# Sums of squares on TensorE and lo parts on VectorE in the opening of a hybrid RWKV-7/FoX trunk kernel

## The chip, the core and the metric

The kernel runs on one core of one Trainium2 chip. A core has a matrix engine (TensorE, "PE"; its weight loads are listed apart as "PEld"), a vector engine (VectorE, "DVE"), an engine for activation functions (ScalarE, "ACT"), a general engine (GpSimd, "POOL") and an engine that mostly issues DMAs (SyncE, "SP"). Each engine works through its own list of instructions in order, and they wait for each other through semaphores. The metric is the time of one execution on the device, in microseconds.

All matrix products with weights are made to nearly fp32 accuracy out of three products of a faster format, fp32r. An operand is split into a high part, `hi` (the value rounded to fp32r, a copy on ScalarE), and a low part, `lo` (the value less `hi`, a subtraction on VectorE or GpSimd); then `hi*hi + hi*lo + lo*hi` is summed up in PSUM. Operands that are plain fp32 go through TensorE in another way, in which each product is recorded as two.

## The reference, cut to what matters

One layer: 16 meta tokens are put ahead of 512 tokens of width 1024; the combined input projection feeds an RWKV-7 group, a forgetting-attention group (FoX) and the gates.

```python
h = jnp.concatenate([meta_b, x], axis=1)              # 528 x 1024
u = rmsnorm(h, norm_mix[l])                           # h * rsqrt(mean(h*h) + 1e-6) * g
proj = u @ w_in[l]
feat_rw, feat_fx = proj[..., :C_RW], proj[..., C_RW:C_RW + C_FX]
...
# RWKV-7, after the token shift: r, k, v, wd, ad (64 + 64 columns), gd (128 columns)
w_log = -jax.nn.softplus(-(w0 + jnp.tanh(wd) @ w_lora_up)) - DECAY_OFFSET
a = jax.nn.sigmoid(a0 + ad @ a_lora_up)
g = jax.nn.sigmoid(gd) @ g_lora_up
...
# FoX: fl are 8 columns, one for each head
F = jnp.cumsum(jax.nn.log_sigmoid(fl + b_f))
```

The opening computes the sums of squares for `rmsnorm`, the feature blocks wd/ad ("LoRA block") and gd ("gate LoRA block"), the eight forget columns and their cumulative sum F, and the normalised `u` as hi and lo part for all projections that follow. Behind it come the recurrence, the attention, the output projections and an MLP.

## The kernel before

The activations stand transposed: 1024 channels as 8 blocks of 128 partitions (`k`), and the 528 tokens as two halves of 264 (`t`). The input arrives as `xt[t]`, four pieces of two channel blocks each (`c`), by SP's DMA queue, with the weights of the two LoRA blocks (`wraw`) queued between them.

For each half t the opening does the following.

- For each piece c: ScalarE squares it into `sq` (L340; three buffers). For its two channel blocks ScalarE makes `uhi`, the gained but not yet normalised value (L343), and VectorE makes `ulo` (L344). VectorE adds the two squares up into `acc` (L347 for the first piece, L350 twice for each other one).
- TensorE forms `pf`, the eight forget columns, from `uhi`, `ulo` and the split weights `wf` (L355, 24 products). Then it multiplies `acc` with a matrix of ones, so that every partition gets the sum over all channels (`pss`, L358, one plain fp32 product).
- ScalarE makes the reciprocal root `rs` out of it, by Ln and Exp (L360, L361). VectorE scales `pf` by it into `f0` (L363).
- `proj(B_LORA, ...)` multiplies the half with the LoRA weights (L293, 24 products into a `pj` buffer; there are two). The evacuation scales by `rs` (L369), makes a scaled copy `tm` on ScalarE (L306) and combines them in the token shift into `lf` (L307).

Then `proj(B_GD, ...)` does the same for the gate LoRA block, both halves. After that the normalised values replace the others: VectorE scales `xt` (L379), ScalarE casts it into `uhi` (L381), VectorE subtracts (`ulo`, L382).

The forget columns go through bias, log-sigmoid and a cumulative scan (L395 to L401) into `fF`, which is stored to `fF_d` (L402) and later read by the attention (`nF`). `fF` shares its buffer with `lc`, the scan of the first decay (L693); `f0` shares that of `tha`. Then the LoRA features get tanh (L407) and the gate features a sigmoid by tanh (L408, L409), and both are split into `lhi` and `llo` (L261, called from the lines behind). The first decay uses `lhi` and `llo` of the LoRA block in TensorE's products L688.

ScalarE's functions come in tables: Ln and Exp lie in one, tanh in another, and each change is an instruction ACT_TABLE_LOAD.

After the opening a planner written in Python (`Clock`, `Turns`) interleaves the streams: recurrence, attention, FoX features, and, as filler, the projections of 40 blocks. It estimates when operands are ready and sets TensorE's order by that; the other engines' order is set by a scheduler with priorities. `projections` fetches a block's weights (L440), splits them in `convert` (hi on ScalarE, L449; lo on GpSimd, L450), and multiplies (L478, 24 products for each half into a `pj` buffer, of which there are two). The first blocks are those of the first pair's keys (`okk`) and receptances (`orr`); the sums for the keys' norm are L710. A `pj` buffer is free again when `tm` (L306) and the token shift (L307) have read it.

`load_w(src, low)` fetches two halves of a block and splits them through `load_h`; `low` says which engine makes the two lo parts, and without it that is VectorE. For the two LoRA blocks `(G, G)` is given: GpSimd, L237.

Of the kernel before, what the change touches and what calls it, by code (L numbers as in the profile page):

```python
# [9 lines left out]
F32 = mybir.dt.float32  # L10
# [3 lines left out]
AF = mybir.ActivationFunctionType  # L14
ALU = mybir.AluOpType
# [4 lines left out]
T = 528  # L20
# [5 lines left out]
HT = T // 2  # L26
# [22 lines left out]
B_LORA = 0  # L49
B_GD = 1  # L50
# [138 lines left out]
def kernel(ctx, tc, ht, x, win, par, cst, gain, lora, wout, wo, wup, wdn, out, dbg=None):  # L189
    nc = tc.nc  # L190
    dbg = dbg or {}
    mm = nc.tensor.matmul
    act = nc.scalar.activation
    V, G, A = nc.vector, nc.gpsimd, nc.scalar
# [35 lines left out]
    def load_h(src, low, tag, bufs):  # L230

        raw = wp.tile([128, 512], F32, name=tag + "raw", bufs=bufs[0])
        nc.sync.dma_start(raw, src)
        hi = wp.tile([128, 512], F32R, name=tag + "hi", bufs=bufs[1])
        lo = wp.tile([128, 512], F32R, name=tag + "lo", bufs=bufs[2])
        A.copy(hi, raw)  # L236
        low.tensor_tensor(lo, raw, hi.bitcast(F32), ALU.subtract)  # L237
        return hi, lo

    def load_w(src, low=(V, V)):  # L240

        return [load_h(src[:, 512 * j:512 * j + 512], low[j], "w", (4, 4, 4)) for j in range(2)]

    def wk(w, k):

        return [x[:, 128 * (k % 4):128 * (k % 4) + 128] for x in w[k // 4]]
# [12 lines left out]
    def split(hi, lo, x):  # L259
        A.copy(hi, x)  # L260
        V.tensor_tensor(lo, x, hi.bitcast(F32), ALU.subtract)  # L261

    def passes(w, x):
        return ((w[0], x[0]), (w[0], x[1]), (w[1], x[0]))
# [6 lines left out]
    with ExitStack() as st:  # L271
# [3 lines left out]
        def ppj(name="ppj"):  # L275
            return ps.tile([128, 512], F32, name=name, tag="pj", bufs=2)

        def psm(name="psm"):
            return ps.tile([128, 512], F32, name=name, tag="sm", bufs=4)
# [5 lines left out]
        def proj(blk, evac, parts=((0, HT), (HT, T)), w=None):  # L285

            w = w or load_w(win[blk], (G, V))
            for a0, a1 in parts:
                po = ppj("pj")[:, :a1 - a0]
                n = 0  # L290
                for k in range(KB):
                    for a, b in passes(wk(w, k), U):
                        mm(po, a, b[:, k, a0:a1], start=n == 0, stop=n == 23)  # L293
                        n += 1
                evac(po, slice(a0, a1))
# [4 lines left out]
        def tshift(blk, dst):  # L300

            tm = rp.tile([128, 1 + T], F32, name="tm")
            V.memset(tm[:, 0:1], 0.0)

            def evac(po, sl):
                act(tm[:, sl.start + 1:sl.stop + 1], po, AF.Copy, scale=pr[:, C_MU + blk:C_MU + blk + 1])  # L306
                V.scalar_tensor_tensor(dst[:, sl], po, pr1[:, blk:blk + 1], tm[:, sl], ALU.mult, ALU.add)  # L307
            return evac
# [5 lines left out]
        lhi = cp.tile([128, 2, T], F32R, name="lhi")  # L314
        llo = cp.tile([128, 2, T], F32R, name="llo")
# [2 lines left out]
        f0 = rp.tile([8, T], F32, name="f0", tag="tha")  # L318
        f1 = rp.tile([8, T], F32, name="f1", tag="sq")
        lfs = [rp.tile([128, TP], F32, name=f"lf{i}", tag=("okk", "orr")[i]) for i in range(2)]  # L320
        with tc.tile_pool(name="xp", bufs=2) as xp:
            ones = xp.tile([128, 128], F32, name="ones", bufs=1)
            V.memset(ones, 1.0)
            xt = [yp.tile([128, KB, HT], F32, name=f"xt{t}", tag=("y_rw", "y_fx")[t]) for t in range(2)]
            nc.sync.dma_start(pr, par)
            for c in range(4):
                nc.sync.dma_start(xt[0][:, 2 * c:2 * c + 2, :].rearrange("p a b -> p (a b)"), ht[0, c])
            w_lora = load_w(win[B_LORA], (G, G))
            for c in range(4):
                nc.sync.dma_start(xt[1][:, 2 * c:2 * c + 2, :].rearrange("p a b -> p (a b)"), ht[1, c])  # L330
            w_gd = load_w(win[B_GD], (G, G))
            nc.sync.dma_start(cs, cst)
            wf = [xp.tile([128, 64], F32R, name=f"wf{i}", bufs=1) for i in range(2)]
            split(wf[0], wf[1], pr[:, C_FL:])
            rss = []
            for t in range(2):
                tk = slice(HT * t, HT * t + HT)
                for c in range(4):
                    sq = xp.tile([128, 2, HT], F32, name="sq", bufs=3)
                    act(sq, xt[t][:, 2 * c:2 * c + 2, :], AF.Square)  # L340
                    for k in range(2 * c, 2 * c + 2):
                        gn = pr[:, C_GN + k:C_GN + k + 1]
                        act(uhi[:, k, tk], xt[t][:, k, :], AF.Copy, scale=gn)  # L343
                        V.scalar_tensor_tensor(ulo[:, k, tk], xt[t][:, k, :], gn, uhi[:, k, tk].bitcast(F32), ALU.mult, ALU.subtract)  # L344
                    if c == 0:
                        acc = xp.tile([128, HT], F32, name="acc")
                        V.tensor_tensor(acc, sq[:, 0, :], sq[:, 1, :], ALU.add)  # L347
                    else:
                        for k in range(2):
                            V.tensor_tensor(acc, acc, sq[:, k, :], ALU.add)  # L350
                pf = psm("pf")[:8, :HT]
                n = 0
                for k in range(KB):
                    for a, b in passes([x[:, 8 * k:8 * k + 8] for x in wf], U):
                        mm(pf, a, b[:, k, tk], start=n == 0, stop=n == 23)  # L355
                        n += 1
                pq = psm("pss")[:, :HT]
                mm(pq, ones, acc, start=True, stop=True)  # L358
                rs = xp.tile([128, HT], F32, name="rs")
                act(rs, pq, AF.Ln, bias=eps, scale=1.0 / 1024)  # L360
                act(rs, rs, AF.Exp, scale=-0.5)  # L361
                rss.append(rs)
                V.tensor_tensor(f0[:, tk], pf, rs[:8], ALU.mult)  # L363
                if t == 0:
                    V.tensor_scalar(pr1, pr[:, C_MU:C_MU + 14], -1.0, 1.0, ALU.mult, ALU.add)
                    shift = tshift(12 + B_LORA, lfs[0])

                def normed_shift(po, sl):
                    V.tensor_tensor(po, po, rss[sl.start // HT], ALU.mult)  # L369
                    shift(po, sl)  # L370

                proj(B_LORA, normed_shift, ((tk.start, tk.stop),), w_lora)
            shift = tshift(12 + B_GD, lfs[1])
            proj(B_GD, normed_shift, w=w_gd)
            for t in range(2):
                tk = slice(HT * t, HT * t + HT)
                for c in range(4):
                    for k in range(2 * c, 2 * c + 2):
                        V.scalar_tensor_tensor(xt[t][:, k, :], xt[t][:, k, :], pr[:, C_GN + k:C_GN + k + 1], rss[t], ALU.mult, ALU.mult)  # L379
                    kk = slice(2 * c, 2 * c + 2)  # L380
                    A.copy(uhi[:, kk, tk], xt[t][:, kk, :])  # L381
                    V.tensor_tensor(ulo[:, kk, tk], xt[t][:, kk, :], uhi[:, kk, tk].bitcast(F32), ALU.subtract)  # L382
# [20 lines left out]
        dump("F", fF)  # L403


        lf, gf = (x[:, :T] for x in lfs)
        act(lf[:64], lf[:64], AF.Tanh)  # L407
        act(gf, gf, AF.Tanh, scale=0.5)  # L408
        V.tensor_scalar(gf, gf, 0.5, 0.5, ALU.mult, ALU.add)  # L409
        split(lhi[:, B_LORA, :], llo[:, B_LORA, :], lf)  # L410
        split(lhi[:, B_GD, :], llo[:, B_GD, :], gf)

        fp = st.enter_context(tc.tile_pool(name="fp", bufs=1))
# [22 lines left out]
        def fetch(job):  # L436
# [4 lines left out]
                raws.append(raw)  # L441
            return job, raws

        def convert(job, raws):
            w = []
            for raw in raws:
                hi = wp.tile([128, 512], F32R, name="whi", bufs=4)
                lo = wp.tile([128, 512], F32R, name="wlo", bufs=4)
                A.copy(hi, raw)  # L449
                G.tensor_tensor(lo, raw, hi.bitcast(F32), ALU.subtract)  # L450
                w.append((hi, lo))
            return job, w

# [594 lines left out]
    with ExitStack() as st:  # L1048
# [35 lines left out]
        for j in range(2):  # L1084
            we = yp.tile([128, 2, 2, 512], F32R, name=f"we{j}", tag=("y_rw", "y_fx")[j])
            for x in range(2):
                raw = wp.tile([128, 512], F32, name="wraw", bufs=4)
# [5 lines left out]
        for b2 in range(4):  # L1093
            w = load_w(wo[0, b2])
            for i, b1 in [(i, b1) for b1 in range(2) for i in range(4)] if b2 < 3 else [(i, b1) for i in range(4) for b1 in range(2)]:
                k = 2 * b2 + b1
                for n, (a, b) in enumerate(passes(M, w[b1])):
                    mm(pd[i], a[:, k, 128 * i:128 * i + 128], b, start=k == 0 and n == 0, stop=k == 7 and n == 2)
        for k in range(KB):
            raw = wp.tile([128, 512], F32, name="wraw", bufs=4)  # L1100
# [265 lines left out]
```

## Time and profile before

| | us |
|---|---|
| three runs | 919.47, 911.35, 915.79 |
| their median | 915.79 |
| the profiled execution | 918.31 |
| its span | 916.5 |

Busy over the span: TensorE 860.8 us (94%), VectorE 601.1 (66%), ScalarE 464.6 (51%), GpSimd 187.7 (20%). The granted clock of TensorE has a mean of 0.969 of full speed.

How to read the lines that follow. A line of the timeline gives the start, the time taken, engine, source line, operation, the tile written and those read, shape and count, and in brackets how long the engine had been idle and what ended that. Where a count is over 1, the time is that from the first start to the last end. An instruction may start before the one ahead of it ends, so the step from start to start is the price of one in a dense stretch. A line of the windows gives a stretch and its length, then busy time and number of instructions of PE, PEld, DVE, ACT and POOL, the granted clock of TensorE, the busy share of the DMA engines and GB/s. A line of the groups gives the count, then busy time and mean nanoseconds of one, then the idle time before. The chain of waits gives start, length, and what the time went to.

### The profile page before, as it was taken

Reading aid. Unit: us, or ns where it says so; the run is one execution under the profiler, and the core shown is the slowest. Engines: PE = TensorE matmul, PEld = TensorE weight load, DVE = VectorE, ACT = ScalarE, POOL = GpSimd, SP = SyncE. Lnnn points to the kernel's source line nnn. Section 1 sums busy time; section 2 is a strip of 40 time slices with the busy share of each in tenths; the row PEclk is TensorE's granted clock in tenths of the full one; section 3 lists DMA queues with packets and bytes.
Section 4 is the critical chain, followed back from the end, with each engine's and each line's share of the span. In section 5 each row is a group of like instructions: output and inputs, shape, how many; then the busy total and the mean of one; then the engine's idle time right before and its main releaser. Section 6 shows DMA issues by size and latency. Waiting matters only on the chain.

```text
span 916.5 us, 15714 instructions
## 1 busy us (share of the span) xinstructions
PE 860.8 (94%) x5868; PEld 699.9 (76%) x5868; DVE 601.1 (66%) x1174; ACT 464.6 (51%) x939; POOL 187.7 (20%) x177
## 2 busy tenths in 40 slices
PE   6589897999989899999999999999999999999998
PEld 4587785867887777767867877888888888888886
DVE  7966875555877697465366756467556675566776
ACT  7756342585545443467364645245544454344542
POOL 4253533314533345222401210000000000000000
PEclk9889988999989899999997999999999999999999
DMA  6122634748464546665686644024632356422465
GB/s 209 46 71 70 161 94 136 185 105 209 105 140 117 138 133 188 174 161 138 152 218 218 213 164 128 1 79 131 193 126 93 104 178 194 156 96 101 137 222 170
DMA packets 69772, 129.46 MB, mean 141 GB/s; under 512 B 6840, under 2 KB 7992, under 8 KB 69696
## 3 DMA queue, kind: packets, MB, share of 16 engines
q1 hardware_dynamic: 52288, 94.91, 32.0%
q0 software_dynamic: 8704, 16.78, 11.4%
q10 hardware_dynamic: 8704, 16.78, 5.5%
q8 instruction: 46, 0.75, 0.3%
q14 instruction: 30, 0.25, 0.1%
HBM read 122.13 MB, written 39.86 MB: 177 GB/s over the span
## 4 chain that ended last, share of the span: by engine, by line
PE 72%; DVE 16%; DMA 4%; ACT 4%; issue 3%; POOL 0%; POOLq 0%; SPq 0%; ACTq 0%; DVEq 0%
PE po L1145 19%; PE pj L478 17%; PE po L1235 12%; PE pd L1235 5%; PE po L1066 2%; PE po L1115 2%; DMA wraw<-in_win 2%; PE pw L830 2%; PE py L627 1%; PE psc L582 1%; DVE tmp L812 1%; DVE AX L824 1%; PE pbt L778 1%; DVE xt L379 1%; PE psr L763 1%
## 5 line engine op out<-in xcount | busy, mean ns | idle before, releaser
L237 DVE TENSOR_TENSOR wlo<-wraw,whi 128x512 fp32r<-128x512 f32 x196 | 138.3, 713 | 95.4 <-ACT whi L236 95.3
L236 ACT CAST whi<-wraw 128x512 fp32r<-128x512 f32 x200 | 123.7, 621 | 134.8 <-PE po L1145 43.9
L478 PE MATMUL pj<-uhi,whi 128*128 128x264 f32 (+1 forms) x480 | 170.9, 356 | 10.4 <-ACT gt L489 4.7
L478 PE MATMUL pj<-uhi,wlo 128*128 128x264 f32 (+1 forms) x480 | 158.5, 330 | 0.0
L478 PE MATMUL pj<-ulo,whi 128*128 128x264 f32 (+1 forms) x480 | 158.4, 330 | 0.0
L450 POOL TENSOR_TENSOR wlo<-wraw,whi 128x512 fp32r<-128x512 f32 x80 | 110.3, 1389 | 173.9 <-ACT whi L449 155.4
L478 PEld LDWEIGHTS pj<-uhi,whi 128*128 128x128 f32 x480 | 94.3, 197 | 31.9 <-issue 11.6
L478 PEld LDWEIGHTS pj<-uhi,wlo 128*128 128x128 f32 x480 | 94.7, 197 | 7.2
L478 PEld LDWEIGHTS pj<-ulo,whi 128*128 128x128 f32 x480 | 95.0, 198 | 4.2
L1145 PE MATMUL po<-zhi,whi 128*128 128x512 f32 (+1 forms) x248 | 94.8, 382 | 0.0
L1145 PE MATMUL po<-zlo,whi 128*128 128x512 f32 (+1 forms) x248 | 94.8, 382 | 0.0
L1145 PE MATMUL po<-zhi,wlo 128*128 128x512 f32 (+1 forms) x248 | 94.8, 382 | 0.0
L449 ACT CAST whi<-wraw 128x512 fp32r<-128x512 f32 x80 | 49.4, 618 | 52.4 <-PE pj L478 29.8
L1235 PE MATMUL po<-wlo,fhi 128*128 128x512 f32 x160 | 62.3, 390 | 0.0
L1235 PE MATMUL po<-whi,flo 128*128 128x512 f32 x160 | 62.3, 390 | 0.0
L1235 PE MATMUL po<-whi,fhi 128*128 128x512 f32 x160 | 62.2, 389 | 0.0
L1145 PEld LDWEIGHTS po<-zlo,whi 128*128 128x128 f32 x248 | 46.6, 188 | 9.1
L1145 PEld LDWEIGHTS po<-zhi,wlo 128*128 128x128 f32 x248 | 46.6, 188 | 9.0
L1145 PEld LDWEIGHTS po<-zhi,whi 128*128 128x128 f32 x248 | 46.6, 188 | 9.0
L1157 ACT CAST fhi<-R 128x768 fp32r<-128x768 f32 (+1 forms) x32 | 30.2, 944 | 24.2 <-DVE R L1164 13.6
L1158 DVE TENSOR_TENSOR flo<-R,fhi 128x768 fp32r<-128x768 f32 (+1 forms) x32 | 34.8, 1088 | 7.8 <-ACT fhi L1157 7.8
L1235 PEld LDWEIGHTS po<-wlo,fhi 128*128 128x128 f32 x160 | 30.0, 188 | 6.5 <-DVE wlo L237 0.2
(295 smaller groups left out, 1667.9 us busy)
## 6 DMA issues: line engine op xcount, KB each, us to landing
wraw<-in_win SPq DMA_DIRECT2D x84, 256.0 KB, 3.2
tsum<-in_wdn ACTq DMA_DIRECT2D x32, 512.0 KB, 4.4
wraw<-in_wup SPq DMA_DIRECT2D x64, 256.0 KB, 2.6
wraw<-tsum SPq DMA_DIRECT2D x64, 256.0 KB, 2.8
wraw<-in_wdn SPq DMA_DIRECT2D x48, 256.0 KB, 2.6
tsum<-in_wdn POOLq DMA_DIRECT2D x16, 512.0 KB, 7.4
tsum<-tsum POOLq DMA_DIRECT2D x16, 512.0 KB, 6.7
gd<-gt SPq DMA_DIRECT2D x16, 256.0 KB, 2.4
```

Of the source, the lines that this page charges most:

```text
L236: A.copy(hi, raw)
L237: low.tensor_tensor(lo, raw, hi.bitcast(F32), ALU.subtract)
L449: A.copy(hi, raw)
L450: G.tensor_tensor(lo, raw, hi.bitcast(F32), ALU.subtract)
L478: mm(po, a, b[:, k, a0:a1], start=n == 0, stop=n == 23)
L830: mm(ps_[hs, n - b0, :], lhs(n)[hs], rhs(n)[hs], start=True, stop=True)
L1066: mm(po, a, b[:, k, :], start=n == 0, stop=n == 11)
L1115: mm(po, a[:, k, 128 * i:128 * i + 128], b[:, k, :], start=n == 0, stop=n == 23)
L1145: mm(po[:, t0:t1], a, b[:, k, t0:t1], start=n == 0, stop=n == 23)
L1157: A.copy(fhi[:, j, a:b], R[:, a:b])
L1158: V.tensor_tensor(flo[:, j, a:b], R[:, a:b], fhi[:, j, a:b].bitcast(F32), ALU.subtract)
L1235: mm(x[i], a[:, k, left, 128 * i:128 * i + 128], c, start=start and k == 0 and n == 0, stop=stop and k == n_pairs - 1 and n == 2)
```

## The change

It has three parts.

1. `acc` and its additions are gone. Each square is multiplied with the ones directly and summed up in PSUM: 8 plain fp32 products for each half instead of one, issued behind each piece.
2. The lo parts of the two LoRA blocks' weights and of the first two projection jobs (four tiles each) are made by VectorE instead of GpSimd.
3. Tanh and split of the LoRA features stand ahead of the gate LoRA block instead of behind the cumulative scan.

```diff
@@ opening
+        lf, gf = (x[:, :T] for x in lfs)
...
-            w_lora = load_w(win[B_LORA], (G, G))
+            w_lora = load_w(win[B_LORA])
...
-            w_gd = load_w(win[B_GD], (G, G))
+            w_gd = load_w(win[B_GD])
...
                     if c == 0:
-                        acc = xp.tile([128, HT], F32, name="acc")
-                        V.tensor_tensor(acc, sq[:, 0, :], sq[:, 1, :], ALU.add)
-                    else:
-                        for k in range(2):
-                            V.tensor_tensor(acc, acc, sq[:, k, :], ALU.add)
+                        pq = psm("pss")[:, :HT]
+                    for k in range(2):
+                        mm(pq, ones, sq[:, k, :], start=c + k == 0, stop=c + k == 4)
...
-                pq = psm("pss")[:, :HT]
-                mm(pq, ones, acc, start=True, stop=True)
...
                 proj(B_LORA, normed_shift, ((tk.start, tk.stop),), w_lora)
+            act(lf[:64], lf[:64], AF.Tanh)
+            split(lhi[:, B_LORA, :], llo[:, B_LORA, :], lf)
             shift = tshift(12 + B_GD, lfs[1])
             proj(B_GD, normed_shift, w=w_gd)
@@ behind the cumulative scan
-        lf, gf = (x[:, :T] for x in lfs)
-        act(lf[:64], lf[:64], AF.Tanh)
         act(gf, gf, AF.Tanh, scale=0.5)
         V.tensor_scalar(gf, gf, 0.5, 0.5, ALU.mult, ALU.add)
-        split(lhi[:, B_LORA, :], llo[:, B_LORA, :], lf)
         split(lhi[:, B_GD, :], llo[:, B_GD, :], gf)
@@ projections
+        converted = []
+
         def convert(job, raws):
+            low = V if len(converted) < 2 else G
+            converted.append(job)
...
-                G.tensor_tensor(lo, raw, hi.bitcast(F32), ALU.subtract)
+                low.tensor_tensor(lo, raw, hi.bitcast(F32), ALU.subtract)
```

In the order in which the changed kernel issues, TensorE begins with the six sums of the first three pieces of the first half; then come six pf products, the two sums of the last piece, the other 18 pf products and the LoRA block of that half; then the eight sums, 24 pf products and the LoRA block of the second half; then the gate LoRA block with the L688 products in its last quarter, and L478. On SP the store of `fF` now leaves after six of L440's weight tiles, where it left after eight. ScalarE loads a table three times between the opening's Ln/Exp and the first decay, as before. Past the first decay and the first keys, the lists of all engines are the same in both kernels but for a few neighbours that change places.

## The prediction

> **What bounds the kernel now.** I read the windows of the opening first, then the chain of waits, then each engine's timeline up to 60 us. Times are microseconds from the start of the span. The windows give, for each stretch, the busy time of TensorE (PE), its weight loads (PEld), VectorE (DVE), ScalarE (ACT) and GpSimd (POOL), with counts, and the clock granted to TensorE:
>
> ```profile
> 15.00:20.00 5.00, 3.97 (x34) 3.16 (x33) 4.96 (x10) 5.00 (x12) 2.93 (x2) 1.00 0.27 85
> ...
> 25.00:30.00 5.00, 3.42 (x28) 3.20 (x27) 5.00 (x11) 4.28 (x8) 1.26 (x1) 1.00 0.17 52
> 30.00:35.00 5.00, 2.89 (x23) 2.48 (x21) 5.00 (x12) 4.99 (x10) 1.19 (x1) 1.00 0.01 2
> 35.00:40.00 5.00, 0.00 (x0) 0.00 (x0) 5.00 (x8) 2.11 (x5) 1.79 (x2) 0.75 0.30 105
> 40.00:45.00 5.00, 3.62 (x20) 3.39 (x21) 3.82 (x8) 4.94 (x8) 0.28 (x2) 0.50 0.00 0
> ```
>
> VectorE is full from 15 to 40 us, and TensorE has nothing at all to do in the last five of them; then its clock stands at 0.50. The chain of waits says the same: work of VectorE, one piece after the other, until the split of the LoRA features (L261) lets the first L688 product go:
>
> ```profile
> 10.12 0.52 ACT sq L340
> ...
> 40.09 0.62 DVE ulo L382
> 40.71 0.63 DVE llo L261
> 41.34 0.04 issue
> 41.38 1.47 PE pup L688 x10
> 42.85 11.16 PE pj L478 x72
> ```
>
> So a gain in the opening is worth what it brings forward the stream of L478. Behind the opening all engines of the changed kernel issue in the old order but for a few neighbours, so what is gained there moves the rest as a block.
>
> **What VectorE loses and takes on.** Groups in the first 30 us (count, busy us, mean ns), and from the whole page the subtraction at L237 on VectorE:
>
> ```profile
> L237 POOL TENSOR_TENSOR wlo<-wraw,whi 128x512 fp32r<-128x512 f32 x4 | 5.9, 1506 | 9.4 <-ACT whi L236 9.4
> L350 DVE TENSOR_TENSOR acc<-acc,sq 128x264 f32<-128x264 f32 x12 | 5.1, 428 | 1.3 <-ACT sq L340 1.3
> ...
> L237 DVE TENSOR_TENSOR wlo<-wraw,whi 128x512 fp32r<-128x512 f32 x196 | 138.3, 713 | 95.4 <-ACT whi L236 95.3
> ```
>
> The 14 additions (these twelve and the two of L347, at 0.43: 6.0 us) go. Eight lo parts come: four of L237 and the four of the first two projection jobs, 8 x 0.71 = 5.7 us. On busy time that is nothing. But VectorE is also held up under GpSimd's subtractions:
>
> ```profile
> 17.16 1.91 DVE L344 SCALAR_TENSOR_TENSOR ulo<-xt,pr,uhi 128x264 fp32r<-128x264 f32 x2
> 34.57 2.51 DVE L379 SCALAR_TENSOR_TENSOR xt<-xt,pr,rs 128x264 f32<-128x264 f32 x2
> 37.63 0.48 DVE L379 SCALAR_TENSOR_TENSOR xt<-xt,pr,rs 128x264 f32<-128x264 f32 x1
> ...
> 33.81 2.98 POOL L450 TENSOR_TENSOR wlo<-wraw,whi 128x512 fp32r<-128x512 f32 x2 [7.55 <-ACT whi L449]
> ```
>
> Undisturbed, an instruction takes 0.48; these pairs take 1.91 and 2.51 instead of about 0.9, so 1.0 to 1.6 us are lost each time. With eight subtractions off GpSimd some 5 us of stalls should go too. The Trainium skill, page "SBUF — State Buffer", section "SBUF: two separate sides", has a GpSimd operation and a VectorE one with two SBUF inputs exclude each other for a whole instruction; by that the loss is up to one subtraction each, and these rows agree. VectorE is then no longer the bound, and the question is what is late next.
>
> **What comes next: TensorE.** The sums of squares become 16 plain fp32 products against two before, each recorded as two:
>
> ```profile
> 24.22 0.28 PE L293 MATMUL pj<-ulo,whi 128*128 128x264 f32 x1
> 24.35 0.71 PE L358 MATMUL pss<-acc,ones 128*128 128x264 f32 x2
> 24.71 0.48 PE L293 MATMUL pj<-uhi,wlo 128*128 128x264 f32 x1
> 25.03 0.28 PE L293 MATMUL pj<-uhi,whi 128*128 128x264 f32 x1
> ...
> 47.76 0.28 PE L478 MATMUL pj<-ulo,whi 128*128 128x264 f32 x1
> ...
> 53.72 0.28 PE L478 MATMUL pj<-uhi,wlo 128*128 128x264 f32 x1
> 53.93 1.11 PE L710 MATMUL pkk<-sq,cs 64*64 64x264 f32 x8
> ```
>
> Between 47.76 and 53.72 lie 49 steps of 0.122, the price of one fp32r product. From 24.35 to 25.03 go one sum and one such product, so a sum holds TensorE for 0.68 - 0.12 = 0.56. Bounds: 0.24 (both records at the fp32r pace) and 0.86 (two records of 0.43 one after the other). I take 0.56, the row itself. The Trainium skill, page "FP8 and Floating Point Precision", section "TensorE Precision Notes", counts four passes for true fp32; four times 0.122 is 0.49 as an estimate, and the sum below would be 0.7 us shorter by it.
>
> TensorE's new order is strict: the sums of the first half stand ahead of most of its pf products, those of the second half behind the whole LoRA block of the first half. The last squares of the first half are ready at 10.64, as now (10.12 + 0.52; their input lands no earlier). From there, two sums 1.1; 18 pf products left 2.2; LoRA block 24 x 0.122 = 2.9; eight sums 4.5; pf of the second half 2.9; its LoRA block 2.9; drain 0.3: 27.5. The squares that wait for a free sq buffer (three, now freed by TensorE and not VectorE) are made in time, since the eight sums begin at 16.9.
>
> **Then ScalarE.** From 27.5 its queue is full. These rows price it by start-to-start steps:
>
> ```profile
> 27.67 0.48 ACT L306 ACTIVATE tm<-pj,pr 128x264 f32<-128x264 f32 x1 [0.57 <-DVE pj L369]
> 28.05 0.62 ACT L381 CAST uhi<-xt 128x528 fp32r<-128x528 f32 x1
> 28.57 0.73 ACT L395 ACTIVATE f<-f,pr 8x528 f32<-8x528 f32 x1
> 29.32 1.28 ACT L407 ACT_TABLE_LOAD   x1
> 30.61 0.65 ACT L407 ACTIVATE lf<-lf 64x528 f32<-64x528 f32 x1
> 31.16 0.46 ACT L306 ACTIVATE tm<-pj,pr 128x264 f32<-128x264 f32 x1
> ...
> 40.96 1.28 ACT L398 ACT_TABLE_LOAD   x1
> 42.25 0.64 ACT L398 ACTIVATE f<-f 8x528 f32<-8x528 f32 x1
> ```
>
> VectorE's scaling of the block (0.4) puts the first tm at 27.9. Then, in the changed order: three tm at 0.38, eight uhi casts and the lhi cast at 0.52, one table load 1.29, tanh 0.55, and the first decay's two sg and one small cast, about 1.1 by the tm and cast rows: 8.8. So the load ahead of L398 starts at 36.7 instead of 40.96, 4.3 earlier. The tanh and split moved ahead cost nothing of their own: three table loads before, three after. Its cover is that TensorE meanwhile does the second LoRA block; the L688 products no longer wait until 41.38 but slip in near 32, and L478 starts near 33.8 instead of 42.85.
>
> **And the last wait.** L478 has two pj buffers. Its third batch of 24 must wait until VectorE has evacuated the first (L307, okk). In VectorE's fixed order that stands behind the scan of lc, whose buffer is that of fF, so behind fF's store:
>
> ```profile
> 47.17 1.36 DVE L693 TENSOR_TENSOR_SCAN lc<-smask,sg 128x576 f32<-128x576 bf16 x1 [0.75 <-DMA fF_d<-fF]
> 48.72 0.49 DVE L307 SCALAR_TENSOR_TENSOR okk<-pj,pr,tm 128x264 f32<-128x264 f32 x1 [0.19 <-ACT tm L306]
> ```
>
> Now: load at 40.96, okk done at 49.2, that is 8.2 later. After: the same chain, with about 0.8 more, because the second split (lhi, llo) and two lo parts are now queued between the scan of fF and that of lc: 36.7 + 9.0 = 45.7. The third batch starts at 45.7; now it starts 24 steps before 53.72 + 0.12, at 50.9. TensorE has nothing between the end of the second batch (about 40.5: 33.8, two batches of 2.9, and a wait of under 1 us for the buffer of the LoRA block before) and 45.7. Behind the waiting product stand L710 and all later products.
>
> That gap has a price. TensorE's last products before its present pause, and the clock behind them:
>
> ```profile
> 33.27 0.39 PE L688 MATMUL pup<-lhi,lw 64*128 64x264 f32 x2 [0.76 <-ACT lhi L260]
> ...
> 34.00:36.00 2.00, 0.00 (x0) 0.00 (x0) 2.00 (x4) 1.70 (x4) 2.00 (x2) 1.00 0.00 0
> 36.00:38.00 2.00, 0.00 (x0) 0.00 (x0) 2.00 (x3) 0.63 (x1) 0.80 (x1) 0.87 0.46 157
> 46.00:48.00 2.00, 2.00 (x13) 2.00 (x11) 1.22 (x3) 0.46 (x2) 0.00 (x0) 0.57 0.05 8
> ```
>
> 0.87 in 36 to 38 means a fall at 37.5, some 3.8 us after the last product ended at 33.7; it is back at 47.7, 6.3 us after work resumed at 41.38. In a gap of 5.2 it falls as well. The Trainium skill, page "TensorE: Matmul & The Clock Gate", section "Part 1: The HAM clock gate (the "warmup" mystery)", names one idle window of about 3.4 us for the fall; the trace agrees. At half clock a step is 0.244, the third batch 5.9 instead of 2.9: L710 at 51.6, or at 48.6 with a clock that never fell. I take 51.2, near the cold end, since the clock now needed 6.3 us to come back.
>
> **The sum.** 53.9 - 51.2 = 2.7 us gained, as a block to the end. Two queues are reordered. SP sends fF's store ahead of the seventh and eighth weight tile; how long a tile then takes:
>
> ```profile
> wraw<-in_win SPq DMA_DIRECT2D x84, 256.0 KB, 3.2
> ```
>
> They leave by about 44 and land near 47, for a batch that starts after 55. GpSimd makes the third job's second lo part only after three other operations (dg twice, BK), which start near 46.5; with four times about 1.5, by the row of L237, it is done at 52.5, for products at about 56. Both covers hold by 3 us or more; gone, each would cost what is missing. The profiled execution took 918.31 (span 916.5 and 1.8 around it), 2.5 above the median of the three runs (915.79; 911.35 to 919.47); 915.79 - 2.7 = 913.1. About 1% (9.2 us) is what a measurement of this kernel can tell from no change, so the forecast is "within 1%".
>
> **Rivals.**
> 1. *The gap stays warm or is short.* If L478's second batch ends later or okk earlier, so that the gap is under 3.4 to 3.8, the clock holds: third batch 45.7 + 2.9, L710 at 48.6, gain 5.3: 910.5. For it: only 1.5 us decide. Chance 0.20.
> 2. *No wait for the pj buffer.* If okk's evacuation does not stand behind the fF store, the stream runs on from 33.8 warm: gain 9.0 plus 2.4 for the half clock of now (half of 42.85 to 47.7), 11.4: 904.4. Against it: the fixed order of VectorE. Chance 0.08.
> 3. *The sums cost too much: slower.* Ten sums lie on TensorE's path. At 0.83 each the gain is gone; at the bound of 0.86 each everything from 27.5 on is 3.0 later, L710 at 54.2, 0.3 slower; with ScalarE's chain another microsecond longer, 917. For it: ScalarE must wait for TensorE's sums before Ln and Exp, which every later step needs. Chance 0.20.
> 4. *The gain is given back behind the opening* (the attention's inputs come through ScalarE, and fF's order with the weight tiles on SP has changed): 915.8. Chance 0.10.
> 5. The forecast: 0.42. That the change does not do what it says is excluded: the additions are gone from VectorE's list.
>
> Three runs before spread over 8 us, so a median may be off by 3. The range goes from 906 (rival 1 and that spread; rival 2 left out) to 918.5 (rival 3 and part of the spread). Faster by over 1% needs rival 2, or rival 1 with a favourable spread: 0.09; slower by over 1% needs far more than rival 3: 0.04; within 1%: 0.87.
>
> **What would show it.** VectorE has gaps before 40 us; pss takes about 0.56 a product and Ln of the second half starts near 21.6; L688 runs near 32; the load ahead of L398 starts near 36.7; okk's first L307 ends near 45.7; a TensorE gap of about 5 us ends there, with the clock at 0.50 behind it; L710 at 51.2. Wrong it would be with VectorE still full to 40, with L478 running through, or with L710 at 54.

## The result, and the profile after

| kernel | runs | median us | range us |
|---|---|---|---|
| before | 17 | 917.67 | 911.35 to 923.1 |
| with the change | 17 | 910.17 | 906.3 to 915.47 |

The ratio is 0.9921, with a 95% interval of 0.9898 to 0.9944: 7.5 us, or 0.8%, faster. That is within 1%, as forecast, and the forecast time of 913.1 was 2.9 us too high. Measured twice more, the same kernel came to 0.9918 (0.9889 to 0.9947) and 0.9926 (0.9904 to 0.9947).

The profiled execution of the changed kernel has a span of 904.6 us against 916.5, a difference of 11.9 us. Before one reads anything into so large a difference, one should ask how much of it a second pair of profiles would show; that comes with the experiments. First the opening. The windows of the changed kernel (columns as before: PE, PEld, DVE, ACT, POOL, clock, DMA share, GB/s):

```profile
25.00:30.00 5.00, 5.00 (x44) 5.00 (x43) 4.67 (x11) 4.45 (x8) 0.00 (x0) 1.00 0.31 93
30.00:35.00 5.00, 5.00 (x43) 4.42 (x42) 3.96 (x9) 5.00 (x12) 0.14 (x1) 1.00 0.04 13
35.00:40.00 5.00, 4.92 (x39) 4.57 (x38) 4.24 (x9) 4.94 (x8) 0.00 (x0) 1.00 0.01 3
40.00:45.00 5.00, 0.08 (x1) 0.00 (x0) 4.49 (x8) 4.41 (x10) 1.59 (x3) 0.88 0.38 118
45.00:50.00 5.00, 4.91 (x22) 4.91 (x23) 2.69 (x6) 3.77 (x6) 4.85 (x4) 0.50 0.44 150
```

VectorE has room from 25 us on (4.67, 3.96, 4.24 instead of 5.00 each). In its place TensorE is full up to 40, and ScalarE from 30 on. Then TensorE stands still, and the clock is at 0.50 when it starts again. The steps on the way, from the timeline of the changed kernel (start, time taken, engine, line, operation):

```profile
16.91 3.72 PE L349 MATMUL pss<-sq,ones 128*128 128x264 f32 x16
20.28 0.48 PE L354 MATMUL pf<-uhi,wf 128*8 128x264 f32 x1
20.59 0.29 PE L354 MATMUL pf<-ulo,wf 128*8 128x264 f32 x1
...
20.67 0.48 ACT L357 ACTIVATE rs<-pss,eps 128x264 f32<-128x264 f32 x1 [1.55 <-PE pss L349]
...
31.55 0.39 PE L688 MATMUL pup<-lhi,lw 64*128 64x264 f32 x2
...
36.03 1.28 ACT L397 ACT_TABLE_LOAD   x1
```

The eight sums of the second half are 16 records. From 16.91 to 20.59 go these sums and one fp32r product of `pf`; counted as the prediction counted its single sum, that is (3.68 - 0.12) / 8 = 0.44 us for a sum. (The first `pf` product starts only 0.03 us behind the last record of the sums and the next one 0.31 later, so 3.37 / 8 = 0.42, up to its start, is too little.) The `rs` activation by Ln starts at 20.67, L688 runs at 31.55, and the load ahead of the logarithm of the forget columns (L397 here, L398 before) starts at 36.03. Then the last wait:

```profile
39.39 1.25 DVE L400 TENSOR_TENSOR_SCAN fF<-f,f 8x528 f32<-8x528 f32 x1
40.57 0.40 DVE L406 TENSOR_SCALAR lf<-lf 128x528 f32<-128x528 f32 x1
40.89 0.67 DVE L450 TENSOR_TENSOR wlo<-wraw,whi 128x512 fp32r<-128x512 f32 x1
42.08 0.71 DVE L261 TENSOR_TENSOR llo<-lf,lhi 128x528 fp32r<-128x528 f32 x1 [0.51 <-ACT lhi L260]
42.70 0.68 DVE L450 TENSOR_TENSOR wlo<-wraw,whi 128x512 fp32r<-128x512 f32 x1
43.30 1.35 DVE L693 TENSOR_TENSOR_SCAN lc<-smask,sg 128x576 f32<-128x576 bf16 x1
44.57 0.47 DVE L307 SCALAR_TENSOR_TENSOR okk<-pj,pr,tm 128x264 f32<-128x264 f32 x1
...
45.09 0.59 PE L478 MATMUL pj<-uhi,whi 128*128 128x264 f32 x1 [5.02 <-DVE okk L307]
...
50.67 0.66 PE L710 MATMUL pkk<-sq,cs 64*64 64x264 f32 x4
```

The third batch of L478 starts at 45.09 behind okk's evacuation, after a pause of 5.02 us, and L710 follows at 50.67. Between the two scans VectorE shows no wait for the store of `fF`: what stands there is its own list, with 0.51 us of waiting for ScalarE's `lhi`.

### The profile page after: what moved, and what is told of

Read it like the earlier page. It is cut to its first block, busy times and chain, and to the rows that moved or that the text cites. A ratio compares the mean times of both kernels' runs of the same rounds, so it can differ in the third digit from the quotient of the medians.

```text
span 904.6 us, 15741 instructions
## 1 busy us (share of the span) xinstructions
PE 859.2 (95%) x5896; PEld 699.9 (77%) x5896; DVE 594.3 (66%) x1168; ACT 463.6 (51%) x939; POOL 176.7 (20%) x169
## 4 chain that ended last, share of the span: by engine, by line
PE 70%; DVE 17%; ACT 5%; DMA 4%; issue 3%; POOL 0%; POOLq 0%; SPq 0%; ACTq 0%; DVEq 0%
PE po L1145 19%; PE pj L478 15%; PE po L1235 12%; PE pd L1235 5%; PE po L1115 2%; PE po L1066 2%; PE py L627 1%; PE pw L830 1%; DMA gl<-gd 1%; DVE tmp L812 1%; DVE AX L824 1%; PE pbt L778 1%; PE psc L582 1%; DVE Tt L824 1%; DVE AX L813 1%
## 5 line engine op out<-in xcount | busy, mean ns | idle before, releaser
L237 DVE TENSOR_TENSOR wlo<-wraw,whi 128x512 fp32r<-128x512 f32 x200 | 140.4, 709 | 94.2 <-ACT whi L236 93.9
L478 PE MATMUL pj<-uhi,whi 128*128 128x264 f32 (+1 forms) x480 | 168.9, 352 | 14.1 <-DVE okk L307 5.0
L478 PE MATMUL pj<-uhi,wlo 128*128 128x264 f32 (+1 forms) x480 | 156.8, 327 | 0.0
L478 PE MATMUL pj<-ulo,whi 128*128 128x264 f32 (+1 forms) x480 | 156.5, 326 | 0.0
L450 POOL TENSOR_TENSOR wlo<-wraw,whi 128x512 fp32r<-128x512 f32 x76 | 104.8, 1387 | 156.2 <-ACT whi L449 131.7
L478 PEld LDWEIGHTS pj<-uhi,whi 128*128 128x128 f32 x480 | 92.5, 193 | 35.7 <-issue 11.2
L478 PEld LDWEIGHTS pj<-uhi,wlo 128*128 128x128 f32 x480 | 92.8, 193 | 7.1
L478 PEld LDWEIGHTS pj<-ulo,whi 128*128 128x128 f32 x480 | 93.0, 194 | 4.3
```

## The experiments

The change and all twelve runs behind it, in their order; "before" is the median of the kernel before that was measured beside them, and rows with the same figure share it. "L710" is where those sums start in the profile. "Near 100 us" is the start of a VectorE instruction, the fourth evacuation into `orr`, at 102.3 us in the first profile of before, less the mean of the same instruction in three profiles of the kernel before (these lie 0, -1.1 and -0.1 us from the first of them); its neighbours from 92 us on give the same to 0.1 us. Both columns come from one profile of each run.

| kernel | median us | before us | ratio (95%) | L710 us | near 100 us |
|---|---|---|---|---|---|
| the change | 910.17 | 917.67 | 0.9921 (0.9898 to 0.9944) | 50.67 | -3.4 |
| sums alone | 916.44 | 920.82 | 0.9963 (0.9938 to 0.9987) | 50.97 | -1.5 |
| lo parts alone | 912.10 | 920.82 | 0.9918 (0.9891 to 0.9944) | 50.17 | -5.0 |
| split alone | 921.12 | 920.82 | 1.0005 (0.9984 to 1.0026) | 48.99 | +2.5 |
| the change, 2nd | 912.55 | 920.82 | 0.9918 (0.9889 to 0.9947) | 51.09 | -2.9 |
| without sums | 909.40 | 920.04 | 0.9892 (0.9860 to 0.9924) | 49.55 | -6.0 |
| without lo parts | 915.23 | 920.04 | 0.9943 (0.9914 to 0.9971) | 53.52 | -0.4 |
| forget chain ahead | 910.44 | 920.04 | 0.9887 (0.9856 to 0.9918) | 49.68 | -5.8 |
| before, 2nd | 916.38 | 920.04 | 0.9978 (0.9951 to 1.0005) | 53.25 | -0.7 |
| before, 3rd | 919.32 | 918.05 | 1.0020 (0.9997 to 1.0043) | 53.69 | +0.3 |
| the change, 3rd | 910.96 | 918.05 | 0.9926 (0.9904 to 0.9947) | 50.87 | -3.2 |
| without sums, 2nd | 912.24 | 918.05 | 0.9935 (0.9913 to 0.9956) | 48.94 | -5.1 |
| forget chain, GpSimd | 911.04 | 918.05 | 0.9941 (0.9916 to 0.9966) | 48.93 | -3.6 |

Read the two controls first: an unchanged kernel came out 3.7 us below and 1.3 us above the runs of before beside it. Two kernels a few microseconds apart can't be ranked by one such median.

**Sums alone.** Part 1 of the change, the rest as before:

```diff
-                            V.tensor_tensor(acc, acc, sq[:, k, :], ALU.add)
+                    for k in range(2):
+                        mm(pq, ones, sq[:, k, :], start=c + k == 0, stop=c + k == 4)
```

> Part 1 alone (sums of squares on TensorE; lo parts stay on GpSimd, split stays behind the scan). Theory A (VectorE was the bound of the opening, its list loses 6.0 us of additions; behind the opening nothing structural changes): VectorE is no longer full between 15 and 30 us but still held up by GpSimd's subtractions; the scan of fF ends 2 to 4 us before 45.8, L710 at 50 to 52, time 2 to 4 us below the kernel before. Rival B (the additions were only filler beside the stalls; the stalls under GpSimd's subtractions carried the opening): L710 within 1 us of 53.9, time the same within 2 us. Rival D (sums on TensorE cost more than they free): L710 after 54.5, slower by 1 us or more. A pss product takes 0.42 us as in the whole change.

L710 came at 50.97 and the time 4.4 us lower, so theory A held for the place and rivals B and D fell. A sum takes 0.44 us here too, not 0.42. The scan of fF moved much farther than expected (33.11): the scheduler put the forget chain elsewhere, so more than the sums differs from the kernel before. But the stalls are still there. VectorE's rows in this kernel's timeline:

```profile
17.93 2.98 DVE L344 SCALAR_TENSOR_TENSOR ulo<-xt,pr,uhi 128x264 fp32r<-128x264 f32 x3
...
47.21 0.49 DVE L307 SCALAR_TENSOR_TENSOR okk<-pj,pr,tm 128x264 f32<-128x264 f32 x1 [1.65 <-ACT tm L306]
```

Three instructions that take about 1.3 undisturbed take 2.98 beside a GpSimd subtraction, and near 100 us only 1.5 us are left of the gain.

**Lo parts alone.** Part 2, the rest as before:

```diff
-            w_lora = load_w(win[B_LORA], (G, G))
+            w_lora = load_w(win[B_LORA])
...
+            low = V if len(converted) < 2 else G
```

> Part 2 alone (lo parts of the first weights on VectorE, additions stay there too). Theory A: VectorE takes 5.7 us of busy time and loses about 5 us of stalls, so it stays full from 15 to 40 us and L710 stays within 1 us of 53.9; time within 2 us of the kernel before. Rival B (the stalls carried the opening): the pairs L344 and L379 take 0.9 instead of 1.9 to 2.5 us, L710 comes 3 to 4 us earlier, time 3 to 7 us lower.

Theory A fell. VectorE is as full as before, yet everything comes earlier. Windows of this kernel, then rows of VectorE and TensorE from its timeline:

```profile
30.00:35.00 5.00, 0.39 (x2) 0.19 (x2) 5.00 (x12) 3.28 (x7) 0.00 (x0) 0.69 0.01 2
35.00:40.00 5.00, 2.76 (x16) 2.52 (x17) 5.00 (x9) 4.86 (x6) 0.28 (x2) 0.50 0.08 22
```

```profile
17.41 1.28 DVE L344 SCALAR_TENSOR_TENSOR ulo<-xt,pr,uhi 128x264 fp32r<-128x264 f32 x3
...
31.26 1.70 DVE L379 SCALAR_TENSOR_TENSOR xt<-xt,pr,rs 128x264 f32<-128x264 f32 x4
...
50.17 1.11 PE L714 MATMUL pkk<-sq,cs 64*64 64x264 f32 x8 [0.97 <-ACT sq L709]
```

Three L344 take 1.28 and four L379 1.70. "Busy 5.00" had hidden the difference: an instruction that is held up counts as busy. The work that VectorE takes on is paid for by the stalls that it loses, and 5.0 us are gained near 100 us. Rival B held for the place; the time, 8.7 us lower, fell by more than its 3 to 7.

**Split alone.** Part 3, the rest as before:

```diff
+            act(lf[:64], lf[:64], AF.Tanh)
+            split(lhi[:, B_LORA, :], llo[:, B_LORA, :], lf)
             shift = tshift(12 + B_GD, lfs[1])
```

> Part 3 alone (tanh and split of the LoRA features ahead of the gate LoRA block). Theory A: VectorE still full to 40 us; the L688 products slip in before 38 us, L478 starts earlier than 42.85, but okk's first evacuation still waits behind the scan of lc, so the third batch of L478 and L710 come within 1 us of before (53.9); time within 2 us. Rival B2 (the moved split is what carries the gain): L710 at 51 or earlier, 3 us or more gained.

Neither theory as stated: L710 came 5 us earlier (48.99), and the time did not move. The other chain, which the sum for L710 does not see, is the scan of lc. From this kernel's timeline:

```profile
42.90 1.28 ACT L401 ACT_TABLE_LOAD   x1
...
46.56 1.61 DVE L404 TENSOR_TENSOR_SCAN fF<-f,f 8x528 f32<-8x528 f32 x1
...
48.95 1.28 ACT L255 ACT_TABLE_LOAD   x1
50.24 1.28 ACT L690 ACT_TABLE_LOAD   x1
51.41 1.35 DVE L693 TENSOR_TENSOR_SCAN lc<-smask,sg 128x576 f32<-128x576 bf16 x1
52.41 1.28 ACT L713 ACT_TABLE_LOAD   x1
54.37 1.28 ACT L695 ACT_TABLE_LOAD   x1
56.43 2.76 POOL L740 TENSOR_TENSOR dg<-cs,P 64x576 f32<-64x576 f32 x2 [8.06 <-ACT P L695]
```

L690 (on the L688 products) and L695 (the exponential behind the scan of lc) now fall between activations that need other tables, so ScalarE loads a table four times from 48.95 to 54.37. The scan of lc starts 4.2 us later than before (51.41 against 47.17), and GpSimd has waited 8.06 us for what follows it. That this is where L710's gain is given back is read from this one trace: near 100 us the kernel is 2.5 us late.

**The change again.**

> The whole change once more, for a second profile and more times. Theory A (3.8 us from the opening; of the rest of the profiles' difference most is where the clock of TensorE happens to fall behind the opening): against the kernel before the median is 4 to 8 us lower; L710 again at 50.7 within 0.3, but the clock falls behind 100 us stand at other places or in other number than in the first profile (146.2, 245.2 and 467.1 us). Rival C (structural gain behind the opening): the same clock falls at the same places within 1 us, and the same offset of about 11 us against the kernel before from 320 us on.

L710 at 51.09 (0.1 us outside the 0.3 that was allowed) and the pause (5.04 us) repeat. The falls behind it do not: this profile has falls at 300.8 and 423.7, which the first has not. Its span is 5.0 us under that of the first profile of before, where the first profile of the change was 11.9 under it. Theory A held for the profiles; the median was 8.3 us lower, just above its 4 to 8.

**Without the sums, and without the lo parts.** The change with part 1 undone, and with part 2 undone:

```diff
-                    for k in range(2):
-                        mm(pq, ones, sq[:, k, :], start=c + k == 0, stop=c + k == 4)
+                            V.tensor_tensor(acc, acc, sq[:, k, :], ALU.add)
```

```diff
-            w_lora = load_w(win[B_LORA])
+            w_lora = load_w(win[B_LORA], (G, G))
...
-                low.tensor_tensor(lo, raw, hi.bitcast(F32), ALU.subtract)
+                G.tensor_tensor(lo, raw, hi.bitcast(F32), ALU.subtract)
```

> Parts 2 and 3 without part 1 (VectorE keeps its 14 additions). The runs so far: lo parts alone 8.7 us faster than before, sums alone 4.4, split alone nothing. Theory S (parts 1 and 2 both relieve VectorE and what they free ends at the same next limits, so either one gives nearly all; the split gives nothing): the median lies 5 to 9 us under the kernel before, within 3 us of the whole change. Rival T (they add up, as in the working: additions 6.0 us and stalls 5 us): without the sums at least 3 us of the whole change's gain are gone, and the split, which pushed the scan of fF from 44.3 to 46.6 us when alone, makes it worse: 0 to 4 us under the kernel before.

> Parts 1 and 3 without part 2 (GpSimd keeps the lo parts of the first weights). Theory S: sums alone gave 4.4 us, so this gives 3 to 6 us; scan of lc near 43 to 45 us, as with the whole change. Rival U (the lo parts carry what lies over the opening's 3.8 us, through fewer collisions of GpSimd and VectorE and fewer microseconds at half clock; the sums only duplicate part of it): 0 to 4 us under the kernel before and mean granted clock near 0.971, like the sums alone and the kernel before, not 0.977.

Rival T fell at once: without part 1 nothing was lost (10.6 us under before). Without part 2 the opening's gain is gone: -0.4 us near 100 us, L710 at 53.52. The time was still 4.8 us lower with a mean clock of 0.977, so rival U named the right part but not the way, and theory S had the time but not the reason. A row that shows the stalls, from the timeline without the lo parts: two L345 under a subtraction take 2.95 instead of 0.9.

```profile
15.79 2.95 DVE L345 SCALAR_TENSOR_TENSOR ulo<-xt,pr,uhi 128x264 fp32r<-128x264 f32 x2
```

The scheduler put the forget chain early here as well (scan of fF at 33.27, of lc at 38.19 instead of the 43 to 45 expected), so this variant, like the sums alone, differs from its neighbours in order too, and not in the stalls alone.

The kernel without the sums holds a lesson. Windows of 3.4 us, then two rows of TensorE:

```profile
30.90:34.30 3.40, 0.00 (x0) 0.00 (x0) 3.40 (x9) 2.29 (x4) 0.00 (x0) 1.00 0.00 0
34.30:37.70 3.40, 0.03 (x1) 0.03 (x1) 3.40 (x8) 2.22 (x4) 0.00 (x0) 0.50 0.00 0
37.70:41.10 3.40, 3.40 (x15) 3.40 (x16) 3.34 (x6) 2.78 (x3) 0.14 (x1) 0.50 0.47 154
41.10:44.50 3.40, 3.40 (x30) 3.40 (x29) 1.74 (x4) 1.73 (x4) 0.29 (x2) 1.00 0.47 159
```

```profile
45.93 0.39 PE L482 MATMUL pj<-uhi,whi 128*128 128x264 f32 x1 [0.87 <-DVE okk L307]
...
49.55 1.11 PE L714 MATMUL pkk<-sq,cs 64*64 64x264 f32 x8 [0.42 <-ACT sq L709]
```

Its third batch starts 0.8 us later than that of the change (45.93 against 45.09), and still its sums for the keys' norm come 1.1 us earlier (49.55 against 50.67). It pauses too, and longer, but earlier: half of the time at half clock passes in the pause itself, the clock is back at 41.1, and the third batch runs at full speed.

**The forget chain ahead.** Beside the whole change, the eight forget columns go through bias, log-sigmoid, scan and store before the LoRA features' tanh:

```diff
+            act(f0, f0, AF.Identity, bias=pr[:8, C_BF:C_BF + 1])
...
+            V.tensor_tensor_scan(fF, f0, f1, 0.0, ALU.mult, ALU.subtract)
+            nc.sync.dma_start(fF_d, fF)
             act(lf[:64], lf[:64], AF.Tanh)
```

> The whole change, and besides it the forget columns' chain (bias, log-sigmoid, scan, store) ahead of the LoRA features' tanh and split, so ahead of the gate LoRA block; nothing is left out. Theory A (the last wait of the opening is okk's evacuation behind the scan of lc, which waits for fF's store): Exp and Ln run while their table is still loaded, one change of table and back is saved, the scan of fF ends near 31 us instead of 40.7, lc starts by 39 instead of 43.3, okk's first L307 ends by 41, TensorE's gap of 5.0 us shrinks to under 2, the clock does not fall there, L710 starts at 43 to 46 instead of 50.7. Time 4 to 8 us below the whole change, 11 to 16 below the kernel before. Rival V (another chain is just behind, such as the scan or the inputs of the second decay): L710 earlier, but the time within 2 us of the whole change.

The table change was saved and the scans came early, but okk's evacuation stayed where it was. Windows and VectorE's timeline:

```profile
35.00:40.00 5.00, 3.53 (x28) 3.16 (x26) 5.00 (x10) 3.86 (x10) 1.51 (x2) 1.00 0.31 108
40.00:45.00 5.00, 2.64 (x18) 2.18 (x17) 5.00 (x10) 4.76 (x10) 1.44 (x3) 1.00 0.13 33
```

```profile
30.96 1.23 DVE L376 TENSOR_TENSOR_SCAN fF<-f,f 8x528 f32<-8x528 f32 x1
36.28 1.34 DVE L693 TENSOR_TENSOR_SCAN lc<-smask,sg 128x576 f32<-128x576 bf16 x1
...
39.52 2.91 DVE L389 TENSOR_TENSOR ulo<-xt,uhi 128x528 fp32r<-128x528 f32 x3
...
42.70 1.28 DVE L450 TENSOR_TENSOR wlo<-wraw,whi 128x512 fp32r<-128x512 f32 x2
43.91 0.70 DVE L261 TENSOR_TENSOR llo<-lf,lhi 128x528 fp32r<-128x528 f32 x1
44.53 0.88 DVE L307 SCALAR_TENSOR_TENSOR okk<-pj,pr,tm 128x264 f32<-128x264 f32 x2
```

With lc out of the way at 36.28, okk starts at the same time as without this edit (44.53 against 44.57): VectorE is full from 35 to 45 and reaches it only then. So taking away the wait for fF's store was not enough to move that moment; theory A fell on this point. Part of the full VectorE is stalls again: `dg` on GpSimd needs the scan of lc and so now starts at 38.41, and the three `ulo` beside it take 2.91. TensorE's pause ahead of the third batch did shrink to 1.59 us, as theory A had it, but because the second batch ended late, at 43.47 instead of 40.08, behind waits of 1.47, 0.22 and 0.60 us for VectorE; and the clock fell there all the same, at 45.0. L710 came 1 us earlier, and 910.44 can't be told from the change's own medians, as rival V had it.

**Controls.** The kernel before, unchanged, twice:

> The kernel before once more, for a second profile. Theory A (the falls of the clock behind 100 us that the first profile shows are a matter of where a pause lies against a fixed grid of 3.41 us): the opening's times repeat within 0.5 us (L710 at 53.9, scan of lc at 47.2), but the falls at 112.6, 153.5, 255.9, 307.1 and 477.8 us come in other number or of other length, and the falls all lie whole multiples of 3.41 us apart. Rival C (structural): the same falls at the same places within 1 us.

> The kernel before a third time, as a control in the same call as the whole change: the second time it measured 3.7 us under the kernel before, with which it is identical. Theory N (such a difference is spread between runs, since single executions scatter by 8 to 10 us): within 2 us of the kernel before, to either side. Rival P (kernels that are sent in measure some 3 to 4 us lower than the runs of before that they are compared with, so that much of every gain so far is not the edit's): again 3 to 4 us lower.

The opening repeats: scan of lc at 47.07 and 47.03, L710 at 53.25 and 53.69 (0.7 and 0.2 from the first). The falls differ: only the first profile has one at 112.6, and the second has none near 307. Rival P fell with the third (1.3 us above).

**The change a third time, and without the sums a second time.**

> The whole change a third time, beside the control. The opening in three profiles so far: third batch of L478 at 45.1 to 45.5 us, L710 at 50.7 to 51.1. By the opening alone (theory A) the median lies 3 to 4 us under the control's; if the rest of the 7.5 to 8.3 us measured so far belongs to the edit as well, 7 to 8 under the control's.

> Parts 2 and 3 without part 1 a second time, beside whole change and control. Theory S (part 1 adds nothing once part 2 is there): within 2 us of the whole change. Rival W (the sums on TensorE cost 2 us or more on top of part 2, as 909.4 against 912.6 of two different calls would have it): 2 to 4 us below the whole change. Rival T (they add up): at least 3 us above the whole change.

The change lies 8.4 us under the control and 7.1 under the runs of before: more than the opening gives. Without the sums the kernel is 1.3 us slower than the change this time, so theory S: part 1 neither adds nor costs anything that these runs can tell.

**The forget chain with GpSimd.** As above, with the lo parts of the first two projection jobs left on GpSimd:

```diff
-            low = V if len(converted) < 2 else G
+            low = G
```

> As the variant with the forget columns' chain ahead, but the lo parts of the first two projection jobs stay on GpSimd (those of the two LoRA blocks on VectorE); nothing is left out. In that variant VectorE was full from 35 to 45 us and okk's first evacuation came at 44.5 behind two lo parts (42.7 to 44.0) and the second llo. Theory Q (VectorE's list there is the last limit): 2.8 us less on VectorE, okk's evacuation by 42, the third batch of L478 by 42.5 instead of 45.1, L710 at 46.5 to 48, time 2 to 4 us below that variant and the whole change. Rival R (GpSimd's subtractions hold VectorE up as they did before the change): VectorE still full from 35 to 45, okk's evacuation at 44 or later, time the same or higher than the whole change.

Theory Q fell on its main row, okk's evacuation at 45.28, and R's full VectorE isn't there either. The windows, and the timeline of GpSimd and VectorE:

```profile
40.00:45.00 5.00, 4.33 (x23) 4.11 (x23) 3.75 (x7) 3.81 (x8) 2.38 (x3) 0.66 0.01 3
```

```profile
38.14 2.76 POOL L740 TENSOR_TENSOR dg<-cs,P 64x576 f32<-64x576 f32 x2 [4.58 <-ACT P L695]
38.30 1.56 DVE L389 TENSOR_TENSOR ulo<-xt,uhi 128x528 fp32r<-128x528 f32 x1
...
44.47 0.89 DVE L261 TENSOR_TENSOR llo<-lf,lhi 128x528 fp32r<-128x528 f32 x1 [1.05 <-ACT lhi L260]
45.28 1.03 DVE L307 SCALAR_TENSOR_TENSOR okk<-pj,pr,tm 128x264 f32<-128x264 f32 x2
```

VectorE has room from 40 us on (3.75 of 5.00), and waits 1.05 us for ScalarE's lhi ahead of llo and okk. The other engine has come back in another place: `dg`, which starts early here too, holds up one `ulo` of 0.7 to 1.56, and the products that need it wait 1.03 us. With a wait of 1.02 us ahead of that the clock falls at 41.2 (0.66 in the window shown), and most of the second batch runs at 0.50. Where one limit was moved away others stood close behind: okk's evacuation came 0.75 us later than with the chain ahead alone (45.28 against 44.53). None of the variants was shown to beat the change.

## Why the prediction was right, and where not

**The opening: right, and of the right size.** Over three profiles each, L710 starts at 53.62 before and 50.88 after, 2.74 us earlier; the forecast was 2.7. Step by step, forecast and first profile after: Ln of the second half 21.6 and 20.67; L688 near 32 and 31.55; table load 36.7 and 36.03; third batch 45.7 and 45.09; L710 51.2 and 50.67. The pause, its place and the clock behind it are as described. Rivals 1 to 3 didn't come about: the pause was there, it was long enough for the clock to fall, and the sums cost less than assumed.

**The term that was mis-sized.** "A sum holds TensorE for 0.68 - 0.12 = 0.56" was taken from a single sum between two products of other kinds; eight in a row take 0.44 each. The ten on the path are some 1.1 us cheaper, and Ln of the second half came 0.9 us ahead of the forecast. The Trainium skill, page "FP8 and Floating Point Precision", section "TensorE Precision Notes", with its four passes, gave 0.49 and a third batch 0.7 us earlier, at 45.0. The row says 45.09, so its sum was nearer than mine, though the estimate for one sum was still too high (0.49 against 0.44).

**What carries the gain.** The working counted 6.0 us of additions and 5 us of stalls as VectorE's relief, and then let TensorE and ScalarE set the end. It did not ask whether either alone would do. Either brings L710 to 50.2 to 51.0, and together they reach no farther (50.88), which fits a next limit that is common to both; no run isolates it. The lo parts are the part that lasts: near 100 us they give 5.0 us alone, the sums 1.5, and the change without the lo parts 0.4. The split gave nothing alone; the change without it was not run. The rule of two inputs (the Trainium skill, page "SBUF — State Buffer", section "SBUF: two separate sides") is supported from the other side: three L344 take 2.98 in the kernel with the sums alone, beside a GpSimd subtraction, and 1.28 in that with the lo parts alone, where the subtractions are off GpSimd.

**The wait for fF's store.** "So behind fF's store" was true of the kernel before (0.75 us of waiting in the profile), but not of the kernel after: there the scan of lc starts 2.6 us behind the store's issue (40.67), against 1.6 before, no instruction is recorded as waiting for it, and VectorE's own list fills the time. With the chain moved out of the way okk came at the same moment, though stalls had a part in that. The number came out because the 9.0 us counted the same instructions, the second split and two lo parts among them; the reason given for them did not hold.

**The time: too small a gain.** The forecast time was 2.9 us off, the forecast gain 4.8 (2.7 against 7.5). That the time came nearer is luck: the forecast started from the median of three runs, 915.79, and seventeen runs gave 917.67. The sum stopped at L710, "as a block to the end", with rival 4 taking something away. The reverse happened: three profiles of each kernel, averaged, are 3.2 us apart at 103 us, 4.8 at 121, 6.2 at 234, 7.3 at 440 and 7.5 at 906. Over all runs of the study the medians are 919.0 (109 runs of before) and 911.1 (31 of the change), 7.9 us.

Part of that goes with the clock. The mean granted clock over these runs is 0.9717 before (the 92 of these runs that list one) and 0.9774 after, which is (1 - clock) x 2 x span = 52 and 41 us at half clock. Within the runs of either kernel a microsecond at half clock goes with 0.37 (before) and 0.41 us (after) of time, so 11 us of it would go with about 4.3; that is an estimate, since the two move together and neither was set. In the opening all three profiles of before have 10.2 us at half clock and all three of after 6.8; the other 7 or so are behind it. Why the clock should fall less often there is open. It is not shown that the edit causes it: the change without the lo parts has a clock of 0.977 and the sums alone 0.971, and every changed kernel measured 0.7 to 5.4 us better than its place near 100 us says, the controls 3.0 better and 1.0 worse. The step from 103 to 121 us is mostly one fall in one of the three profiles of before. The 11.9 us between the first two profiles need no explanation of their own.

## What to carry to other kernels

An engine shown as 100% busy may be held up by another: compare the time of the same instruction alone and beside the other engine's work before counting what moving work will cost. Two edits that relieve one engine are not added up, the next limit is looked up first, and one of them alone is tried. Follow every chain that leaves the changed stretch: here the products of L710 could gain 5 us while the scan beside them lost 4, and the time stood still. And take two or three profiles of the unchanged kernel before explaining a difference of 1%.

## What the runs showed of the hardware

The clock falls at the ends of windows on a fixed grid, not at a set time after the last product: the fall in the opening comes 3.8, 2.5 and 3.6 us behind the last product in the three profiles of before, and 3.8, 4.4 and 4.0 in those of the change. In each profile the falls lie whole multiples of 3.41 us apart (after: 43.8, 60.9, 146.2, 245.2, 467.1; 17.1, 102.4, 201.4 and 423.3 are 5, 30, 59 and 124 times 3.41), and the grid lies elsewhere in each execution. The Trainium skill, page "TensorE: Matmul & The Clock Gate", section "Part 1: The HAM clock gate (the "warmup" mystery)", has such a free-running window, and the trace agrees, with 3.41 us; the page lets the clock fall after an idle window, and there the trace differs, for a pause need not fill one. The same pause of 2.3 us, for BK, in the kernel before and after, as windows on each grid:

```profile
303.70:307.10 3.40, 1.08 (x6) 0.59 (x4) 3.16 (x4) 0.16 (x1) 0.94 (x1) 1.00 0.69 157
307.10:310.50 3.40, 3.40 (x17) 2.96 (x18) 1.55 (x3) 3.28 (x5) 1.28 (x1) 0.50 0.65 221
```

```profile
293.00:296.40 3.40, 2.02 (x9) 1.31 (x7) 3.35 (x4) 0.00 (x0) 1.91 (x2) 1.00 0.87 178
296.40:299.80 3.40, 2.33 (x20) 2.04 (x21) 1.85 (x4) 2.58 (x5) 0.36 (x1) 1.00 0.38 117
```

Where it lies in one window (busy 1.08 of 3.40), the clock falls at that window's end. Where the grid cuts it in two (2.02 and 2.33 busy), it doesn't. In the fourteen profiles, behind 12 us, every window at full clock with 2.0 us or more of idle time was followed by a fall; of those between 1.0 and 1.9 some were and some were not. So rival 1's condition, a gap under 3.4 to 3.8 us, was too generous. A pause of 5 us puts at least 2.5 us into one window wherever the grid lies, so that the clock would fall in it was sound; that it takes 3.8 us from the last product was chance. The place of the grid is also part of why executions of one kernel differ: the 92 of before that list a clock lie up to 12.5 us apart, and their time at half clock goes with about two thirds of the variance.
